# A transformer layer's hand-ordered products on one core: subtractions moved from GpSimd to VectorE, evictions spread over steps, bias stores on another queue, a rotation eight steps later

## The chip, the cores and the metric

The kernel runs on one core of a Trainium2 chip. The metric is the device time of one execution in microseconds (us), the median of several. TensorE (PE) multiplies, ScalarE (ACT) and VectorE (DVE) prepare its operands and take its results out of the accumulation banks (PSUM), GpSimd (POOL) and SyncE (SP) mostly issue transfers (DMA); POOL computes a little too.

## What is computed

One layer on 512 tokens of width 2048, batch 1, in float32:

```
h = rmsnorm(x, norm_gain)
aq, ak, av, az, iq, ik, iw, rq, rk, rv, rz, ga, gb = split(h @ w_in)
a_out = dsa_mixer(aq, ak, av, iq, ik, iw, positions, rel_bias) * silu(az)
rq = rope(rq, positions); rk = rope(rk, positions) * 128 ** -0.5
b_out = retention_mixer(rq, rk, rv, ret_gn_gain) * silu(rz)
merged = sigmoid(ga) * (a_out @ w_a_out) + sigmoid(gb) * (b_out @ w_b_out)
r = x + merged @ w_o
out = rmsnorm(r + (p @ w_ple) * sigmoid(r @ w_ple_gate), final_gain)
```

dsa_mixer is attention with 8 heads of 128, where each query uses the 128 keys that an indexer (16 heads of 64) scores highest, plus a bias by relative position. retention_mixer is retention with 8 heads of 128: scores times a decay, a state carried from chunk to chunk, and a group norm.

## The kernel before

**Operands.** TensorE multiplies in the short format fp32r. Each float32 operand is therefore split into a high and a low part, and a product is the sum of three: high by high, high by low, low by high. For a weight tile (128x1024), loaded into one of seven raw buffers, ScalarE writes the high part `wh` (L153) and VectorE the low part `wl` (L158); there are three buffers of each. Some weight tiles are the sum of two blocks: VectorE adds them (L160), or GpSimd issues a load that accumulates in the raw buffer (L119).

**Seven products for eight.** Most projections are computed as pairs of 512 columns by seven block products in place of eight. `combos` (L291) makes the seven operands of h, for 8 steps k: from two tiles xn (normalized at L707) ScalarE writes high parts (L299), the low parts come from a subtraction at L301 or L303, and four sums (L313 to L316) come ahead of them. For h the sums and the low parts of s1, s4 and a22 are GpSimd's, the other low parts VectorE's. The operands are named hs (and ha) in the rows. The parts of the first X_AWAY steps for three of the products (s2, a22, s1) go to memory and are loaded again (`x_load`).

**Order.** No scheduler decides: the program writes each engine's instructions in the order in which they are issued. `step()` is a tick, called after every three matmuls of the value products and after every two in the pairs (56 ticks a pair). `later(n, f)` runs f after n ticks. The list `bg` holds background work (making the parts of h, 48 rounds of the top-k, the masks and matmuls of the bias), of which one entry is taken each `state["rate"]` ticks.

**Stages** on the trace's clock: the indexer's queries up to 106 us; the retention values rv in two passes, 106 to 194 (`values`, L743, four banks, 16 steps; at the end of a pass ScalarE evicts the four banks with `normal`, L764, and issues a store behind each, L892); the attention's values av by seven products, 194 to 272 (`values_pair`, L909; matmuls at L947 to L949). Its results are combined by `value_out` (L896): VectorE adds or subtracts a bank and a copy (L899), ScalarE makes the high part avh, VectorE the low part avl, and ScalarE issues the stores to vd (L906). Two of the four outputs are finished at the end of the last product (`last`). Then 24 pairs, 272 to 790 us: for each of 8 heads one pair of retention query and key columns, then two pairs of merge gates. In `gate_pair` the results of a pair are copied (L246), combined (L250) and summed into `go` (L967). `finish` for a retention pair is `rotate` (L783): for queries (i = 0) and keys (i = 1) ScalarE copies the halves crosswise into `rb` (L786, L787), VectorE does two products and a sum (L788 to L790) 3, 5 and 7 ticks later; behind the keys come the steps of retention (queries times decay, L797; scores, L804; and so on) at fixed ticks, while the gate pairs run. Then the gate and attention pairs up to 1100, the attention, the output projection and the last gate.

**Bias.** The masks mk (L666) are VectorE's; the matmuls' results go through ScalarE into bev (L685), and SP issues the 32 stores to scr (L689), 8 + 4n ticks later. SP also issues most weight loads.

Of the kernel before, what the change touches and what calls it, by code (L numbers as in the profile page):

```python
# [9 lines left out]
F32 = mybir.dt.float32  # L10
F32R = mybir.dt.float32r
# [6 lines left out]
L = 512  # L18
# [17 lines left out]
def block_kernel(tc, xT, pT, posb, posq, w_in, w_v, w_ik, w_a, w_b, w_o, w_ple, w_gate,  # L36
# [4 lines left out]
    with contextlib.ExitStack() as ctx:  # L41
# [10 lines left out]
        def U(name, dt=F32):  # L52
            return up.tile([128, L], dt, name=name, tag="u")
# [121 lines left out]
        def later(n, f):  # L175
            if n <= 0:
                return f()
            tick[1] += 1
            heapq.heappush(soon, (tick[0] + n, tick[1], f))
# [108 lines left out]
                if ended[n] == 16 and n in after:  # L288
                    after[n]()

        def combos(lo, hi, name, keep=None, adder=dve, low={}):  # L291


            X = {n: [None] * 8 for n in PRODUCTS}
            T = {}

            def parts(n, k, src, sign=1.0):
                t = U(name + n, F32R)
                act.activation(t[:, LO], src, AF.Copy, scale=sign)  # L299
                if sign > 0:  # L300
                    low.get(n, dve).tensor_sub(t[:, HI], src, t[:, LO].bitcast(F32))  # L301
                else:
                    dve.scalar_tensor_tensor(t[:, HI], src, sign, t[:, LO].bitcast(F32), op0=OP.mult, op1=OP.subtract)  # L303
# [318 lines left out]
        def index_tile(m, ix):  # L622
            if m > 1:
                todo.extend(N3)
            for s in range(2):
                for t in range(1, NT):
                    todo.append(lambda s=s, t=t: index_score(2 * m + s, ix[s], t))

        for m in range(2):
            index_tile(m, ix[m])  # L630
        for m in range(2, 8):
# [49 lines left out]
        def bias_out(b, ps):  # L681
            t, gs = b
            ln = 128 * (t + 1)
            e = U("bev")
            act.activation(e[:, :ln * len(gs)], ps[:, :ln * len(gs)], AF.Copy, scale=d_back)  # L685
            for n, g in enumerate(gs):
                dst = bass.AP(tensor=scr.tensor, offset=scr.offset + 16 * (g % 8) * 1280 + TOFF[t],
                              ap=[[1280, 16], [128 * 1280, NH], [1, ln]])
                later(8 + 4 * n, lambda dst=dst, n=n: sp.dma_start(dst, e[:, ln * n:ln * n + ln]))  # L689

        def bias_banks(banks):
            for b, ps in [(b, bias_mm(b)) for b in banks]:
                bias_out(b, ps)

        x_away = [(n, k) for k in range(X_AWAY) for n in PRODUCTS[4:]]
        hd = dp.tile([len(x_away), 128, L], F32, name="hd")
        x_at = {nk: hd[i] for i, nk in enumerate(x_away)}
        xn = {}

        def xn_load(k):  # L700
            for i in (k, k + 8):
                xn[i] = U("xn")
                sp.dma_start(xn[i], xT[:, i, :])

        def xn_norm(k):
            for i in (k, k + 8):
                dve.scalar_tensor_tensor(xn[i], xn[i], ng[:, i:i + 1], R["b"], op0=OP.mult, op1=OP.mult)  # L707

        Xh, h_step = combos(lambda k: xn[k], lambda k: xn[k + 8], "h", lambda n, k: x_at.get((n, k)), pool,
                            {n: pool for n in ("s1", "s4", "a22")})  # L710
        bg.append(lambda: xn_load(0))
        for k in range(8):
            if k < 7:
                bg.append(lambda k=k: xn_load(k + 1))
            bg.append(lambda k=k: xn_norm(k))
            bg.extend([lambda k=k, i=i: h_step(k, i) for i in range(X_STEPS)])

        bg.append(lambda: state.update(rate=BG_RATES[1]))
        for r in range(16):
            for t in range(1, NT):  # L720
                bg.append(lambda r=r, t=t: topk_round(t, r == 15))
        bg.append(lambda: state.update(rate=BG_RATES[4]))
# [39 lines left out]
        def normal(ps, name, t, dt=F32):  # L762
            v = U(name, dt)
            act.activation(v, ps, AF.Copy, scale=R["nat"][:, t:t + 1])  # L764
            return v
# [6 lines left out]
        def retention(h):  # L772
# [10 lines left out]
            def rotate(i, o):  # L783
                E[i] = o
                b = U("rb")
                act.activation(b[0:64, :], o[64:128, :], AF.Copy)  # L786
# [94 lines left out]
        x_wanted = collections.deque(x_away)  # L881

        def x_load(s):
            if s >= KT - len(x_away) and x_wanted:
                n, k = x_wanted.popleft()
                Xh[n][k] = U("h" + n, F32R)
                sp.dma_start(Xh[n][k].bitcast(F32), x_at[n, k])

        for i in range(2):
            pss = values(u_rv[i], "rv", x_load if i else lambda s: None)  # L890
            for t, ps in enumerate(pss):
                act.dma_start(rd[i, t], normal(ps, "rv", t))  # L892
        state["rate"] = BG_RATES[2]


        def value_out(i, t, f, x, y):  # L896

            a = U("av")
            f(a, x, y)  # L899
            if t == NT - 1:  # L900
                vs = [(6, a)]
            else:
                h, l = split(a, "av", 2)
                vs = [(2 * t, h.bitcast(F32)), (2 * t + 1, l.bitcast(F32))]
            for j, v in vs:
                later(10 + 2 * (j % 2), lambda j=j, v=v: act.dma_start(vd[i, j], v))  # L906

        def values_pair(ids):
            banks = {}  # L909
# [4 lines left out]
                for j in range(2):  # L914
                    act.activation(E[n][j], banks[b][j], AF.Copy)

            def out(f, b, n, i, half):
                for j in range(2):
                    value_out(i, 2 * half + j, f, banks[b][j], E[n][j])
# [14 lines left out]
            for n, b in enumerate("vpqrpvp"):  # L934
                if b not in banks:
                    banks[b] = [P("ps_v" + b) for _ in range(2)]
                seq = ksteps(ids[n])
                for s, (i, k) in enumerate(seq):
                    if k == 0:
                        split_to(i + AHEAD)  # L940
                        load_to(i + AHEAD + LOADS)
                    h, l = loaded[i]
                    x = Xh[PRODUCTS[n]][s]
                    for j in range(2):
                        a, c = x[:, tok(j)], x[:, tok(2 + j)]
                        o = banks[b][j]
                        pe.matmul(o, a, h[:, k], start=(n < 4 and s == 0), stop=False, skip_group_check=True)  # L947
                        pe.matmul(o, a, l[:, k], start=False, stop=False, skip_group_check=True)
                        pe.matmul(o, c, h[:, k], start=False, stop=(s == 7), skip_group_check=True)  # L949
# [5 lines left out]
        state["rate"] = BG_RATES[3]  # L955


        sgb, sga, mbs = (dp.tile([16, 128, L], F32, name=n) for n in ("sgb", "sga", "mbs"))
# [26 lines left out]
        state["rate"] = BG_RATES[5]  # L985
        for n, u in enumerate(u_rz):
            y = B("y2")

# [402 lines left out]
AHEAD = 3  # L1391
LOADS = 5
BG_RATE = 4
BG_RATES = (2, 3, 5, 24, 16, 8)
X_AWAY = 4
HEAD = 13
WARM = 10
MANUAL = True
# [96 lines left out]
```

## Time and profile before

| | us |
|---|---|
| timed runs | 1680.54, 1682.5, 1682.78; median 1682.5 |
| profiled execution, its own time | 1680.43 |
| span of that execution | 1678.7 |
| idle of TensorE at the start (ps_ikw 1.0 and 0.2, warm 1.4) | 2.6 |
| idle of TensorE in the tail (ps_b on rl of GpSimd) | 3.5 |

TensorE's granted clock is 1.00 in all 40 slices. In the rows, a time in front is the start in us from the start of the span, then comes the duration in us, the engine and the line, the operation, result and operands, the shape, and in square brackets the idle time of the engine just before, with what ended it. A name with q (ACTq) is the engine's sequencer issuing a transfer. A grouped row has the count behind the x, then busy us and mean ns. A row of one source line has the duration in ns as least, median and greatest. The ends of matmuls are modelled; their starts are what counts.

### The profile page before, as it was taken

Reading aid. Unit: us, or ns where it says so; the run is one execution under the profiler, and the core shown is the slowest. Engines: PE = TensorE matmul, PEld = TensorE weight load, DVE = VectorE, ACT = ScalarE, POOL = GpSimd, SP = SyncE. Lnnn points to the kernel's source line nnn. Section 1 sums busy time; section 2 is a strip of 40 time slices with the busy share of each in tenths; the row PEclk is TensorE's granted clock in tenths of the full one; section 3 lists DMA queues with packets and bytes.
Section 4 is the critical chain, followed back from the end, with each engine's and each line's share of the span. In section 5 each row is a group of like instructions: output and inputs, shape, how many; then the busy total and the mean of one; then the engine's idle time right before and its main releaser. Section 6 shows DMA issues by size and latency. Waiting matters only on the chain.

```text
span 1678.7 us, 24639 instructions
## 1 busy us (share of the span) xinstructions
PE 1660.2 (99%) x9160; PEld 1441.5 (86%) x9160; DVE 1300.1 (77%) x1984; ACT 880.0 (52%) x1296; POOL 284.3 (17%) x288
## 2 busy tenths in 40 slices
PE   9999999999999999999999999999999999999997
PEld 7988788888888888888888888888888888888896
DVE  7798988988988887887887777787668887864453
ACT  7465544555555555555555555566633445463342
POOL 2116611111111111111331111100000111112222
PEclk9999999999999999999999999999999999999999
DMA  7427989788788788788998888898466788733222
GB/s 288 127 91 236 321 234 268 174 218 218 181 210 220 178 232 230 168 229 227 248 235 219 218 223 218 247 373 284 162 210 193 196 216 218 208 108 101 88 63 101
DMA packets 125577, 343.26 MB, mean 204 GB/s; under 512 B 13713, under 2 KB 25873, under 8 KB 125457
## 3 DMA queue, kind: packets, MB, share of 16 engines
q1 hardware_dynamic: 90400, 235.22, 41.5%
q0 software_dynamic: 23680, 85.99, 28.1%
q10 hardware_dynamic: 11376, 20.47, 3.4%
q8 instruction: 72, 1.18, 0.3%
q14 instruction: 49, 0.39, 0.1%
HBM read 300.21 MB, written 41.42 MB: 204 GB/s over the span
## 4 chain that ended last, share of the span: by engine, by line
PE 89%; DVE 4%; ACT 2%; issue 2%; POOL 2%; DMA 1%; ACTq 0%; SPq 0%; POOLq 0%; DVEq 0%
PE ps_p L283 23%; PE ps_v L283 15%; PE ps_r L283 8%; PE ps_q L283 7%; PE ps_w L213 3%; PE ps_w L214 3%; PE ps_w L215 3%; PE ps_pg L215 3%; PE ps_pg L213 3%; PE ps_pg L214 3%; PE ps_iq L213 1%; PE ps_iq L215 1%; PE ps_iq L214 1%; DVE wl L158 1%; ACT wh L153 1%
## 5 line engine op out<-in xcount | busy, mean ns | idle before, releaser
L158 DVE TENSOR_TENSOR wl<-wraw,wh 128x1024 fp32r<-128x1024 f32 (+2 forms) x459 | 565.4, 1241 | 156.6 <-ACT wh L153 155.4
L153 ACT ACTIVATE wh<-wraw 128x1024 fp32r<-128x1024 f32 (+2 forms) x459 | 474.3, 1043 | 257.9 <-DVE wraw L160 120.3
L119 POOL DMA_DIRECT2D wraw<-w_in x120 | 106.1, 962 | 644.1 <-DVE mk L666 245.3
L283 PE MATMUL ps_p<-hs,wh 128*128 128x512 f32 x640 | 161.1, 394 | 0.0
L246 ACT ACTIVATE e<-ps_p 128x512 f32<-128x512 f32 x144 | 86.1, 598 | 136.7 <-PE ps_p L283 134.3
L283 PEld LDWEIGHTS ps_p<-hs,wh 128*128 128x128 f32 x640 | 114.9, 189 | 21.3 <-issue 0.7
L283 PE MATMUL ps_p<-hs,wl 128*128 128x256 f32 x640 | 92.1, 284 | 1.6 <-DVE wl L158 1.6
L283 PEld LDWEIGHTS ps_p<-hs,wl 128*128 128x128 f32 x640 | 83.0, 192 | 2.1 <-DVE wl L158 2.0
L283 PE MATMUL ps_r<-hs,wh 128*128 128x512 f32 x320 | 79.9, 392 | 1.3 <-ACT wh L153 1.3
L119 POOL DMA_DIRECT2D wraw<-w_o x24 | 21.1, 945 | 348.5 <-DVE wl L158 316.5
L283 PE MATMUL ps_q<-ha,wh 128*128 128x512 f32 x320 | 80.1, 392 | 0.0
L283 PE MATMUL ps_v<-ha,wh 128*128 128x512 f32 x320 | 80.0, 392 | 0.0
L283 PE MATMUL ps_p<-ha,wh 128*128 128x512 f32 x320 | 79.3, 390 | 0.0
L283 PE MATMUL ps_v<-hs,wh 128*128 128x512 f32 x320 | 79.0, 389 | 0.0
L215 PE MATMUL ps_pg<-rh,wl 128*128 128x512 f32 x192 | 74.8, 390 | 0.0
L214 PE MATMUL ps_pg<-rl,wh 128*128 128x512 f32 x192 | 74.7, 389 | 0.0
L213 PE MATMUL ps_pg<-rh,wh 128*128 128x512 f32 x192 | 74.7, 389 | 0.0
L967 DVE TENSOR_TENSOR go<-e_t 128x256 f32<-128x256 f32 x160 | 68.0, 425 | 6.8 <-DMA bd<-go 1.2
L283 PEld LDWEIGHTS ps_r<-hs,wh 128*128 128x128 f32 x320 | 59.6, 188 | 15.8 <-ACT wh L153 2.9
L283 PEld LDWEIGHTS ps_p<-ha,wh 128*128 128x128 f32 x320 | 59.9, 188 | 12.9 <-issue 0.5
L283 PEld LDWEIGHTS ps_v<-hs,wh 128*128 128x128 f32 x320 | 60.1, 188 | 12.5
L283 PEld LDWEIGHTS ps_v<-ha,wh 128*128 128x128 f32 x320 | 59.5, 188 | 12.1
(409 smaller groups left out, 3739.9 us busy)
## 6 DMA issues: line engine op xcount, KB each, us to landing
wraw<-w_in SPq DMA_DIRECT2D x172, 512.0 KB, 5.3
wraw<-w_in POOLq DMA_DIRECT2D x120, 512.0 KB, 8.0
wraw<-w_v SPq DMA_DIRECT2D x32, 512.0 KB, 4.2
wraw<-w_o SPq DMA_DIRECT2D x32, 512.0 KB, 4.8
wraw<-w_o POOLq DMA_DIRECT2D x24, 512.0 KB, 7.0
wraw<-w_gate SPq DMA_DIRECT2D x24, 512.0 KB, 4.0
wraw<-w_b SPq DMA_DIRECT2D x16, 512.0 KB, 5.9
wraw<-w_a SPq DMA_DIRECT2D x16, 512.0 KB, 4.1
```

The costliest lines, as they stand in the source:

```text
L119: pool.dma_start(out=view(raw_tiles[r], nk, cols), in_=src[:, k0:k0 + nk, :], accum_op=OP.add)
L153: act.activation(h, raw, AF.Copy)
L158: dve.tensor_sub(l, raw, h.bitcast(F32))
L213: pe.matmul(o, h[:, k, w], a, start=(s == order[0]), stop=False)
L214: pe.matmul(o, h[:, k, w], b, start=False, stop=False)
L215: pe.matmul(o, l[:, k, w], a, start=False, stop=(s == order[-1]))
L246: act.activation(E[n], src, AF.Copy)
L283: pe.matmul(o[:, c], w[:, k], X[PRODUCTS[n]][k][:, c], start=(n < 4 and first and k == 0), stop=(ended[n] == 16), skip_group_check=True)
L967: dve.tensor_add(o[:, q], c0, c1)
```

## The change

- `combos` has VectorE do all sums and low parts, for h too.
- The evictions of rv are spread: result t of a pass is evicted and stored 3t ticks after the pass.
- In `values_pair` the four results behind the last product come at ticks 4, 10, 16 and 24 of what follows, their high parts 6 and low parts 9 ticks later, their stores 16 and 18 ticks later; high and low part lie in one big buffer (128x1280) and not in two of the 69 small ones. The earlier results have their parts 2 and 3 ticks later and stores as before.
- The 32 bias stores are issued by GpSimd, 14 + 4n ticks later and not 8 + 4n.
- The keys' rotation is 8 ticks later, the steps of retention 6 ticks later.
- X_AWAY is 5 for 4 (15 tiles for 12); the reloads start at step 3 of the second rv pass and go on in `values_pair`. The background rate of 3 between the parts of h and the top-k is gone; four empty entries stand there.

```diff
-        def combos(lo, hi, name, keep=None, adder=dve, low={}):
+        def combos(lo, hi, name, keep=None):
...
-                    low.get(n, dve).tensor_sub(t[:, HI], src, t[:, LO].bitcast(F32))
+                    dve.tensor_sub(t[:, HI], src, t[:, LO].bitcast(F32))
...
-                adder.tensor_sub(t2[:, LO], x[:, LO], x[:, HI])
-                adder.tensor_sub(t1[:, LO], x[:, HI], y[:, HI])
-                adder.tensor_sub(t1[:, HI], x[:, LO], t1[:, LO])
-                adder.tensor_sub(t2[:, HI], y[:, LO], t1[:, HI])
+                dve.tensor_sub(t2[:, LO], x[:, LO], x[:, HI])
+                dve.tensor_sub(t1[:, LO], x[:, HI], y[:, HI])
+                dve.tensor_sub(t1[:, HI], x[:, LO], t1[:, LO])
+                dve.tensor_sub(t2[:, HI], y[:, LO], t1[:, HI])
...
-                later(8 + 4 * n, lambda dst=dst, n=n: sp.dma_start(dst, e[:, ln * n:ln * n + ln]))
+                later(14 + 4 * n, lambda dst=dst, n=n: pool.dma_start(out=dst, in_=e[:, ln * n:ln * n + ln]))
...
-        Xh, h_step = combos(lambda k: xn[k], lambda k: xn[k + 8], "h", lambda n, k: x_at.get((n, k)), pool,
-                            {n: pool for n in ("s1", "s4", "a22")})
+        Xh, h_step = combos(lambda k: xn[k], lambda k: xn[k + 8], "h", lambda n, k: x_at.get((n, k)))
...
-        bg.append(lambda: state.update(rate=BG_RATES[1]))
...
+        bg.extend([lambda: None] * 4)
+        bg.extend(rounds)
...
-                act.activation(b[0:64, :], o[64:128, :], AF.Copy)
-                act.activation(b[64:128, :], o[0:64, :], AF.Copy)
-                later(3, lambda: dve.tensor_mul(o, o, ct))
-                later(5, lambda: dve.tensor_mul(b, b, st))
-                later(7, lambda: dve.tensor_add(o, o, b))
+                def swap():
+                    act.activation(b[0:64, :], o[64:128, :], AF.Copy)
+                    act.activation(b[64:128, :], o[0:64, :], AF.Copy)
+                n = 8 * i
+                later(n, swap)
+                later(n + 3, lambda: dve.tensor_mul(o, o, ct))
+                later(n + 5, lambda: dve.tensor_mul(b, b, st))
+                later(n + 7, lambda: dve.tensor_add(o, o, b))
                 if i:
                     for n, f in steps:
-                        later(n, f)
+                        later(n + 6, f)
...
-            if s >= KT - len(x_away) and x_wanted:
+            if s > 2 and x_wanted:
...
-            pss = values(u_rv[i], "rv", x_load if i else lambda s: None)
-            for t, ps in enumerate(pss):
-                act.dma_start(rd[i, t], normal(ps, "rv", t))
+            for t, ps in enumerate(values(u_rv[i], "rv", x_load if i else lambda s: None)):
+                later(3 * t, lambda i=i, t=t, ps=ps: act.dma_start(rd[i, t], normal(ps, "rv", t)))
...
+            if big:
+                b = B("avhl", F32R)
+                h, l = b[:, 0:L], b[:, L:2 * L]
             else:
-                h, l = split(a, "av", 2)
+                h, l = U("avh", F32R), U("avl", F32R)
+            later(lags[0], lambda: act.activation(h, a, AF.Copy))
+            later(lags[1], lambda: dve.tensor_sub(l, a, h.bitcast(F32)))
+            later(lags[2], lambda: store(2 * t, h.bitcast(F32)))
+            later(lags[2] + 2, lambda: store(2 * t + 1, l.bitcast(F32)))
...
-                out(dve.tensor_sub, "p", "pv", 1, 1)
-                out(dve.tensor_add, "r", "e3", 1, 0)
+                out(dve.tensor_sub, "p", "pv", 1, 1, (4, 10), (6, 9, 16), True)
+                out(dve.tensor_add, "r", "e3", 1, 0, (16, 24), (6, 9, 16), True)
...
+                    x_load(8 * n + s + 4)
...
-BG_RATES = (2, 3, 5, 24, 16, 8)
-X_AWAY = 4
+BG_RATES = (2, 5, 24, 16, 8)
+X_AWAY = 5
```

More of the change, by code (lines that the diff above doesn't have):

```diff
@@ L627, in index_tile, with xn_load, xn_norm, x_steps @@
                     todo.append(lambda s=s, t=t: index_score(2 * m + s, ix[s], t))
+        x_away = [(n, k) for k in range(X_AWAY) for n in PRODUCTS[4:]]
+        hd = dp.tile([len(x_away), 128, L], F32, name="hd")
+        x_at = {nk: hd[i] for i, nk in enumerate(x_away)}
+        xn = {}
+        def xn_load(k):
+            for i in (k, k + 8):
+                xn[i] = U("xn")
+                sp.dma_start(xn[i], xT[:, i, :])
+        def xn_norm(k):
+            for i in (k, k + 8):
+                dve.scalar_tensor_tensor(xn[i], xn[i], ng[:, i:i + 1], R["b"], op0=OP.mult, op1=OP.mult)
+        Xh, h_step = combos(lambda k: xn[k], lambda k: xn[k + 8], "h", lambda n, k: x_at.get((n, k)))
+        def x_steps(k):
+            load = [lambda: xn_load(k + 1)] if k < 7 else []
+            return load + [lambda: xn_norm(k)] + [lambda i=i: h_step(k, i) for i in range(X_STEPS)]
         for m in range(2):
@@ L889, in block_kernel, with value_out, store @@
         for i in range(2):
[L890 to L896 removed]
+            for t, ps in enumerate(values(u_rv[i], "rv", x_load if i else lambda s: None)):
+                later(3 * t, lambda i=i, t=t, ps=ps: act.dma_start(rd[i, t], normal(ps, "rv", t)))
+        state["rate"] = BG_RATES[1]
+        def value_out(i, t, f, x, y, lags, big=False):
             a = U("av")
             f(a, x, y)
+            h, l = None, None
+            def store(j, v):
+                act.dma_start(vd[i, j], v)
             if t == NT - 1:
[L901 to L906 removed]
+                return later(lags[2], lambda: store(6, a))
+            if big:
+                b = B("avhl", F32R)
+                h, l = b[:, 0:L], b[:, L:2 * L]
+            else:
+                h, l = U("avh", F32R), U("avl", F32R)
[3 more added lines that the diff above has]
+            later(lags[2] + 2, lambda: store(2 * t + 1, l.bitcast(F32)))
         def values_pair(ids):
@@ L915, in copy, with out @@
                     act.activation(E[n][j], banks[b][j], AF.Copy)
-            def out(f, b, n, i, half):
+            def out(f, b, n, i, half, at=(0, 0), *rest):
                 for j in range(2):
-                    value_out(i, 2 * half + j, f, banks[b][j], E[n][j])
+                    later(at[j], lambda j=j: value_out(i, 2 * half + j, f, banks[b][j], E[n][j], *(rest or ((2, 3, 10),))))
             def last():
                 copy("e3", "p")
-                out(dve.tensor_sub, "p", "pv", 1, 1)
-                out(dve.tensor_add, "r", "e3", 1, 0)
+                out(dve.tensor_sub, "p", "pv", 1, 1, (4, 10), (6, 9, 16), True)
+                out(dve.tensor_add, "r", "e3", 1, 0, (16, 24), (6, 9, 16), True)
             after = {
@@ L954, in block_kernel @@
         values_pair(u_av)
-        state["rate"] = BG_RATES[3]
+        state["rate"] = BG_RATES[2]
         sgb, sga, mbs = (dp.tile([16, 128, L], F32, name=n) for n in ("sgb", "sga", "mbs"))
@@ L984, in block_kernel @@
                 gate_pair(u_g[n], to(d[m:m + 2], AF.Sigmoid))
-        state["rate"] = BG_RATES[5]
+        state["rate"] = BG_RATES[4]
         for n, u in enumerate(u_rz):
```

22 lines of the change are left out of this document (3 added, 19 removed).

## The prediction

> **What bounds the kernel now.** First the page: the span and the busy times.
>
> ```profile
> span 1678.7 us, 24639 instructions
> PE 1660.2 (99%) x9160; PEld 1441.5 (86%) x9160; DVE 1300.1 (77%) x1984; ACT 880.0 (52%) x1296; POOL 284.3 (17%) x288
> ```
>
> TensorE is busy for 1660.2 of 1678.7 us. The change neither adds nor drops a matmul, so all that it can win or lose is time in which TensorE stands still; 18.5 us of it are there at all, and those at the start and in the tail (the table of before) are out of reach. So the second view is the list of what TensorE waited for, here the rows that lie between 190 and 500 us:
>
> ```profile
> PE ps_p L283 <- DVE wl L158: 1.6, 2, 1.3
> PE ps_vv L948 <- DVE wl L158: 1.5, 2, 0.8
> PE ps_vv L947 <- ACT wh L153: 1.4, 1, 1.4
> ...
> PE ps_r L283 <- ACT wh L153: 1.3, 3, 0.6
> ```
>
> The columns are microseconds in total, times, longest. That is 5.8 us in eight waits. A wait costs more than its idle time, as the timeline of TensorE at the start of the value products shows:
>
> ```profile
> 194.68 0.39 PE L947 MATMUL ps_vv<-wh,hs 128*128 128x512 f32 x1
> 195.86 0.50 PE L948 MATMUL ps_vv<-wl,hs 128*128 128x512 f32 x1 [0.79 <-DVE wl L158]
> 196.20 0.40 PE L949 MATMUL ps_vv<-wh,hs 128*128 128x512 f32 x1
> ...
> 198.29 0.40 PE L949 MATMUL ps_vv<-wh,hs 128*128 128x512 f32 x1
> 200.07 0.50 PE L947 MATMUL ps_vv<-wh,hs 128*128 128x512 f32 x1 [1.38 <-ACT wh L153]
> ```
>
> Starts are 0.23 us apart when nothing is late (2.09 us for the nine steps from 196.20 to 198.29). From 198.29 to 200.07 pass 1.78, so the wait of 1.38 takes 1.55 beyond the ordinary step, 0.17 more than its idle time, and the first step after a wait takes 0.34 (195.86 to 196.20), another 0.11. So each wait costs its idle time and some 0.28 us: 5.8 + 8 x 0.28 = **8.0 us to be had at most**. The rest of the waits, in the gate pairs:
>
> ```profile
> 284.52 0.74 PE L283 MATMUL ps_p<-hs,wl 128*128 128x256 f32 x4 [1.30 <-DVE wl L158]
> ...
> 301.16 0.74 PE L283 MATMUL ps_r<-hs,wh 128*128 128x512 f32 x2 [0.62 <-ACT wh L153]
> ...
> 306.26 1.22 PE L283 MATMUL ps_p<-hs,wl 128*128 128x256 f32 x8
> ...
> 495.39 1.21 PE L283 MATMUL ps_p<-hs,wl 128*128 128x256 f32 x8 [0.33 <-DVE wl L158]
> ```
>
> The first is in the first pair (282 to 284), the others in the pair behind a head's retention pair (301 us is head 0, 495 head 3; the other two waits of ps_r are in heads 1 and 3, 0.27 and 0.40, with 0.62 the 1.3 of the list).
>
> **The change part by part.**
>
> *Evictions of the retention values, in steps.* ScalarE before the 1.38 wait:
>
> ```profile
> 194.54 0.67 ACT L764 ACTIVATE rv<-ps_vn,r_nat 128x512 f32<-128x512 f32 x1
> 195.24 0.33 ACTq L892 DMA_DIRECT2D rd<-rv  x1
> ...
> 198.97 2.01 ACT L153 ACTIVATE wh<-wt 128x1024 fp32r<-128x1024 f32 x2 [0.40 <-ACT rv L764]
> ```
>
> Four evictions, each with its store behind it, hold ScalarE from 194.54 to 198.97; only then comes the high part that TensorE wants at 198.52, and its low part follows on VectorE. With one eviction each third tick (a tick is three matmuls, 0.69 us, so about 2 us) the high part is behind one eviction, not four, 3 x 1.1 = 3.3 us earlier. That takes the 1.38 wait and the 0.76 behind it (the rest of 1.5 less 0.79). The 0.79 at 195.86 is VectorE's, which is next. The three are 1.4 + 1.5 idle and 3 x 0.28: **-3.75**.
>
> *Sums and low parts on VectorE alone.* 56 GpSimd subtractions (128x256) move to VectorE: 4 sums and 3 low parts in each of 8 steps, all between 106 and 196 us. VectorE there:
>
> ```profile
> 106.00:194.00 88.00, 88.00 (x397) 73.19 (x396) 77.97 (x92) 47.20 (x94) 56.19 (x59) 1.00 0.70 222
> 194.00:272.00 78.00, 75.07 (x329) 61.26 (x328) 63.65 (x106) 38.19 (x45) 13.17 (x16) 1.00 0.92 251
> ```
>
> (busy time of PE, PEld, DVE, ACT, POOL, then the clock, the share of the DMA engines and GB/s). VectorE is busy for 77.97 of 88 us: there is no room for 56 more at the durations that it has now. But these durations are not its own:
>
> ```profile
> L158 DVE TENSOR_TENSOR wl<-wraw,wh 128x1024 fp32r<-128x1024 f32 x13 | 20.3, 1564 | 6.9 <-ACT wh L153 6.9
> ...
> L301 DVE TENSOR_TENSOR hs<-t,hs 128x256 fp32r<-128x256 f32 x16 | 13.9, 890 | 0.0
> L303 DVE SCALAR_TENSOR_TENSOR ha<-xn,ha 128x256 fp32r<-128x256 f32 x8 | 7.9, 990 | 0.0
> L301 DVE TENSOR_TENSOR ha<-xn,ha 128x256 fp32r<-128x256 f32 x8 | 7.1, 889 | 0.0
> ```
>
> The same line, on the same shapes, at 1240 to 1318 us, where GpSimd does nothing, and a low part of weights at 304.99:
>
> ```profile
> L301 DVE TENSOR_TENSOR ms<-t,ms x32: 414/417/419, 1240.6 to 1318.5; 128x256 fp32r<-128x256 f32 x32
> ```
>
> ```profile
> 304.99 1.22 DVE L158 TENSOR_TENSOR wl<-wraw,wh 128x1024 fp32r<-128x1024 f32 x1
> ```
>
> So beside GpSimd an operation takes 890 to 990 ns for 417, and 1564 for 1220. Without GpSimd: the four groups now take 20.3 + 13.9 + 7.9 + 7.1 = 49.2 us; then 13 x 1.22 + 32 x 0.417 = 29.2, and the 56 new ones 56 x 0.417 = 23.4. VectorE goes from 77.97 to 77.97 - 49.2 + 29.2 + 23.4 = **81.4 of 88 us**. It fits, with 3.4 us more work and no operation waiting on a GpSimd sum of 0.8 to 1.1 us; the low parts are then in time at 194.68. I cost it at nothing beyond the wait above. That it fits hangs on GpSimd's being the cause; the other end is the rival B.
>
> *Results of the value products taken out in steps.* ScalarE ahead of the wait at 284.52:
>
> ```profile
> 278.32 2.81 ACTq L906 DMA_DIRECT2D vd<-avl  x3
> ...
> 282.15 1.06 ACT L153 ACTIVATE wh<-wraw 128x1024 fp32r<-128x1024 f32 x1
> ```
>
> Three stores take 2.81 us of its queue, waiting for low parts that VectorE gives late. The high part at 282.15 and its low part (282.10 + 8 x 0.12 is when TensorE wants it) are late by that. With two ticks (0.7 us) and more between an operation and its store, and with the four results spread over 24 ticks (some 8 us) the high part comes up to 2.8 us earlier: **-1.57** (1.30 + 0.27). The same operations are done as before, in larger buffers; they lie beside the matmuls of the first pair, and the banks r and p are wanted again only by its second and later products. If they were not, one bank held for another 24 ticks would cost up to 8 us; I keep that out, since the list of waits of before has no wait for a bank.
>
> *Rotation of the keys later.*
>
> ```profile
> 361.88 0.63 ACT L786 ACTIVATE rb<-go 64x512 f32<-64x512 f32 x1 [2.63 <-DVE go L967]
> ...
> 363.18 1.06 ACT L153 ACTIVATE wh<-wraw 128x1024 fp32r<-128x1024 f32 x1
> ```
>
> ScalarE stood idle for 2.63 us for the sum of VectorE, did two copies, and only then, at 363.18, the high part for which TensorE waited in head 1. In the changed order this high part stands ahead of the copies, in the idle 2.63 us. That takes the three waits of ps_r: 1.3 + 3 x 0.28 = 2.1, and 0.1 for head 2, where the same step is late by less than the list shows: **-2.2**. The wait at 495.39 (0.33 + 0.28 = 0.6) is on VectorE's low part and can go or stay.
>
> What is late next? In head 0 the low part at 304.99 ends at 306.21 and TensorE takes it at 306.26: 0.05 to spare. When the wait of 0.62 + 0.28 goes, TensorE is there 0.9 earlier. In VectorE's changed order the same operations stand ahead of this low part as before (three of the rotation, one decay product, a weight part, a round of the top-k, only in another order; the round is one form smaller in heads 0 and 3, one larger in 1 and 2). So if VectorE's chain doesn't move up, head 0 gives back 0.85 + 0.11, head 3 keeps its 0.6 and gives back its 0.7, and heads 1 and 2 give up to 0.5 back: 2.8 in all. If the chain moves up with TensorE, 0, and the 0.6 of head 3 goes too. I take **+1.0** beyond a kept 0.6, between these ends.
>
> *Bias stores from GpSimd's queue, 6 ticks later.* 32 issues leave SP's queue, where each waits for its eviction ahead of weight loads; no TensorE wait hangs on it: 0. They now stand among GpSimd's accumulating weight loads:
>
> ```profile
> L119 POOL DMA_DIRECT2D wraw<-w_in x80: 857/882/1207, 543.4 to 1079.9; - x80
> ```
>
> 80 x 0.9 + 32 x 0.9 = 101 us in some 540: room enough, so 0 (rival C has the other end). The Trainium skill, "SBUF — State Buffer", section "Summary: rules for kernel authors", speaks against this part: a transfer issued from GpSimd has its descriptors written by GpSimd, which is starved while VectorE runs in its fast modes, and should go from ScalarE's or SP's queue. The row's 857 to 1207 beside the masks' rows bears it out by at most 0.35 us an issue; 32 x 0.35 = 11 us of GpSimd by that rule, and none of TensorE's while the accumulations have slack.
>
> *Five steps of parts to memory and back, not four; the first top-k rate dropped.* Three more tiles of 256 KB out, and back by 13 loads in the second values pass and two in the next stage: 0.5 MB more at 251 GB/s is 2 us of DMA in the 78, share 0.92 to 0.95. Cost 0; the other end is rival D. The top-k and the bias come about one round (8 to 16 us) later, far ahead of the attention at 1100: 0.
>
> **Sum**: -3.75 - 1.57 - 2.2 + 1.0 = -6.5 us; the profiled execution's 1680.4 becomes 1673.9. It lies 2.1 us under the median of the runs shown, so I take the difference from that median: 1682.5 - 6.5 = **1676.0**.
>
> **The rivals.**
> A. VectorE's low part binds in all four heads, one more operation of 128x512 late in each (4 x 0.69 = 2.8): -3.7, **1678.8**. For: 0.05 to spare in head 0. Against: same operations ahead of it.
> B. GpSimd is not what doubles VectorE's durations in that stage. Then the 56 take 890 ns like their neighbours there, 49.8 us, and VectorE has 127.8 us of work in 88: TensorE is held for 39.8, and the gains outside the stage (2.8) remain: **1719**, slower. It decides from 88 - (77.97 - 49.2) = 59.2 us for 13 weight parts and 88 subtractions: with the weight parts at 1.22, 0.49 us a subtraction. For: all four groups are slow there, and no view shows the conflict of the two engines itself. Against: the x32 row at 417.
> C. Bias stores ahead of accumulations in GpSimd's queue: 16 bursts of about 0.9 us, each past the slack: -6.5 + 14.4, **1690**. Against: 101 of 540 us.
> D. DMA: TensorE now comes 3.8 us earlier into a stage at a share of 0.92, raw weights land late, and 5.3 of the gain are lost: **1681.3**, no difference.
>
> **How the numbers follow.** A difference under 0.2% (3.4 us) can't be told from none: faster is under 1679.1, slower above 1685.9. The forecast has 0.55, A 0.20, B 0.07, C 0.05, D 0.13. Faster: 0.55 + 0.20 = 0.75; same 0.13; slower 0.12. The low end is all waits gone, 1682.5 - 8.0 - 0.6, and a run like the lowest of before: 1673.0 or a little under, 1672.5; the high end takes in A and D to 1681.5 and leaves out B and C.
>
> **What would show it.** Right: the rows of ps_vv gone from the list of waits, and that of ps_r; VectorE's low parts of weights at 1.22 and its subtractions at 417 between 106 and 194 us, busy there 81; GpSimd 57 us less, plus 29 for the stores. The prediction is wrong if VectorE's durations there stay at 890, if TensorE waits for low parts in every head, if weight loads are what ScalarE waits for from 194 to 290, or if TensorE waits show up beside the bias, from 540 on.

## The result, and the profile after

The changed kernel takes 1685.1 us (median of 18 runs, 1682.8 to 1687.8), the kernel before 1682.2 (18 runs, 1678.8 to 1685.1): a ratio of 1.0018, 95% interval 1.0011 to 1.0025. A gain of 6.5 us was forecast; 2.9 us were lost, and the time lies above the range.

The page of the changed kernel, its span and busy times:

```profile
span 1683.3 us, 24637 instructions
PE 1662.9 (99%) x9160; PEld 1444.2 (86%) x9160; DVE 1295.3 (77%) x2040; ACT 879.9 (52%) x1296; POOL 250.0 (15%) x264
```

TensorE's list of waits (us in all, times, longest), the rows of 190 to 500 us:

```profile
PE ps_rs L808 <- DVE go L794: 4.2, 4, 1.3
...
PE ps_vp L960 <- ACT wh L153: 2.8, 1, 2.8
...
PE ps_p L283 <- ACT e L246: 1.1, 1, 1.1
PE ps_vp L961 <- DVE wl L158: 0.8, 1, 0.8
```

All eight waits of before are gone. Seven others stand there: 8.9 us idle for 5.8. By the prediction's own measure (idle time and 0.28 each) that is 8.9 + 7 x 0.28 = 10.9 us for 8.0, and 1.6 us more are lost to TensorE's clock, below: 4.5 us, where the two spans differ by 4.6. The median differs by less (2.9), since the profiled execution of before lies 1.8 us under its own median.

**Between 106 and 194 us** the first part did what was worked out. The stretch, and VectorE's groups in it:

```profile
106.00:194.00 88.00, 88.00 (x397) 73.03 (x396) 74.22 (x150) 49.63 (x99) 5.45 (x6) 1.00 0.75 232
```

```profile
L158 DVE TENSOR_TENSOR wl<-wraw,wh 128x1024 fp32r<-128x1024 f32 x13 | 15.9, 1223 | 6.2 <-ACT wh L153 6.0
L301 DVE TENSOR_TENSOR hs<-t,hs 128x256 fp32r<-128x256 f32 x32 | 11.8, 416 | 0.2 <-ACT hs L299 0.2
L641 DVE SCALAR_TENSOR_TENSOR xn<-xn,g_sb,r_b 128x512 f32<-128x512 f32 x16 | 11.3, 745 | 0.0
L301 DVE TENSOR_TENSOR ha<-xn,ha 128x256 fp32r<-128x256 f32 x16 | 6.7, 420 | 0.6 <-ACT ha L299 0.2
```

Subtractions that took 890 beside GpSimd take 416, weight parts 1223 for 1564, and the normalizations, which the prediction left out, take 745 ns for 980. VectorE does 58 instructions more in 74.22 us where it took 77.97; 81.4 were forecast.

**At 206 us** stands the first new wait. ScalarE, TensorE, and the stretch behind the wait:

```profile
196.07 0.67 ACT L763 ACTIVATE rv<-ps_vn,r_nat 128x512 f32<-128x512 f32 x1
204.45 0.33 ACTq L895 DMA_DIRECT2D rd<-rv  x1
204.88 1.06 ACT L153 ACTIVATE wh<-wraw 128x1024 fp32r<-128x1024 f32 x1 [8.14 <-DMA hs<-hd]
```

```profile
205.99 0.50 PE L960 MATMUL ps_vp<-wh,ha 128*128 128x512 f32 x1 [2.76 <-ACT wh L153]
207.25 0.50 PE L961 MATMUL ps_vp<-wl,ha 128*128 128x512 f32 x1 [0.76 <-DVE wl L158]
```

```profile
208.20:211.60 3.40, 3.40 (x10) 2.62 (x9) 2.79 (x6) 2.58 (x4) 0.00 (x0) 0.50 1.04 421
```

The third eviction of the second pass ends at 196.74; its store is issued at 204.45, 7.7 us later, and the high part behind it in ScalarE's queue is late by that. What released the queue is a reload of the parts of h (hs from hd). The last row is the price on top: for 3.4 us TensorE's clock is 0.50 and its ten matmuls start 0.43 us apart, not 0.23. From 208.06 to 211.71 pass 3.65 us for nine steps that take 2.07: 1.6 us.

Why a store waits for a load is in the changed program's list of instructions (number, line, operation, and what it waits for), here ScalarE's and SyncE's:

```
213 L763 Activation rv_2139<-ps_vn_1642,r_nat_607 128x512 [waits DMAHW7_49]
214 L895 DMACopy rd_1117<-rv_2139 128x512 [waits DMAHW3_49,Activation_49]
215 L153 Activation wh_2151<-wraw_1937 128x1024 [waits DVE_49,PE_49]
...
103 L891 DMACopy hs2_2093<-hd_450 128x512 [waits DMAHW3_49,PE_49]
```

Transfers of ScalarE and SyncE share eight completion counters (DMAHW0 to 7) and take them in turn, and a transfer is issued only when the one before it on its counter has landed. Eight transfers ahead of this store, on counter 3, is a reload (number 103 of SyncE), issued at 185.63:

```profile
185.63 0.32 SPq L891 DMA_DIRECT2D hs<-hd  x1
```

It is the slowest of the reloads. Their source line, from issue to landing:

```profile
DMA to landing us min/median/max: 5.6/11.3/18.7
```

In the kernel before the same line has 4.6/9.6/12.9, for 12 reloads where there are 15 now.

**At 292 us** the same thing stands once more, with a store of the value products that waits for an earlier store of its own (the two stores of the row take 0.33 us each; 2.9 us lie between them):

```profile
287.72 3.62 ACTq L906 DMA_DIRECT2D vd<-avhl  x2
291.38 0.60 ACT L246 ACTIVATE e<-ps_p 128x512 f32<-128x512 f32 x1 [4.04 <-DMA vd<-avhl]
```

**In each of heads 0 to 3** the scores wait for the keys' rotation. TensorE and VectorE in head 0:

```profile
305.34 0.98 PE L283 MATMUL ps_r<-hs,wl 128*128 128x256 f32 x6
307.49 1.13 PE L808 MATMUL ps_rs<-go 128*128 128x128 f32 x8 [1.18 <-DVE go L794]
```

```profile
303.46 0.69 DVE L792 TENSOR_TENSOR go<-go,ct 128x512 f32<-128x512 f32 x1 [0.21 <-ACT rb L788]
304.07 1.22 DVE L158 TENSOR_TENSOR wl<-wraw,wh 128x1024 fp32r<-128x1024 f32 x1
305.20 0.69 DVE L793 TENSOR_TENSOR rb<-rb,st 128x512 f32<-128x512 f32 x1
...
306.67 0.68 DVE L794 TENSOR_TENSOR go<-go,rb 128x512 f32<-128x512 f32 x1
307.26 0.55 DVE L801 TENSOR_TENSOR qt<-go,dect 128x384 f32<-128x384 f32 x1
307.73 1.22 DVE L158 TENSOR_TENSOR wl<-wraw,wh 128x1024 fp32r<-128x1024 f32 x1
```

VectorE is busy without a break from 303.46 on; the sum of the rotation (L794), which now stands behind a weight part and a round of the top-k, ends at 307.35, and TensorE has been at the scores since 306.31.

### The profile page after: what moved, and what is told of

Its sections match the earlier page's. It is cut to its first block, busy times and chain, and to the rows that moved or that the text cites. A ratio compares the mean times of both kernels' runs of the same rounds, so it can differ in the third digit from the quotient of the medians.

```text
span 1683.3 us, 24637 instructions
## 1 busy us (share of the span) xinstructions
PE 1662.9 (99%) x9160; PEld 1444.2 (86%) x9160; DVE 1295.3 (77%) x2040; ACT 879.9 (52%) x1296; POOL 250.0 (15%) x264
## 4 chain that ended last, share of the span: by engine, by line
PE 90%; DVE 3%; DMA 3%; ACT 2%; issue 1%; POOL 0%; SPq 0%; ACTq 0%; POOLq 0%; DVEq 0%
PE ps_p L283 23%; PE ps_v L283 15%; PE ps_r L283 7%; PE ps_q L283 7%; PE ps_w L214 3%; PE ps_w L213 3%; PE ps_w L215 3%; PE ps_pg L215 3%; PE ps_pg L214 3%; PE ps_pg L213 3%; DMA hs<-hd 2%; PE ps_iq L213 1%; PE ps_iq L215 1%; PE ps_iq L214 1%; PE ps_vn L754 1%; PE ps_vn L756 1%
```

## The experiments

The theory on which they rest: the loss has three places, two where a store holds ScalarE's in-order queue until a late transfer has landed, one where a rotation was moved closer to its user. The rivals: the DMA engines are simply full and weights land late; VectorE has too much work at a pair's end in any order. All ratios are to the kernel before on the same chip. The runs are spread over four chips, so where two runs on different chips are compared, the difference is given by the medians and by the ratios.

**The rotation alone.** The kernel before with the change's `rotate` (the diff above).

> The kernel before with the keys' rotation alone as in the change (8 ticks later, retention's steps 6 later). Theory now: VectorE has no idle time from the end of the retention pair on, and the scores are brought 2 ticks nearer to the rotation than it is moved; the waits of ps_r (1.3 us) go and four waits of ps_rs for VectorE's go (about 0.5 to 1.3 each) take their place: 0 to 3 us slower than before. Theory of the prediction: the waits of ps_r go and at most a low part is late: 1 to 2 us faster. Rival: the waits of ps_rs in the changed kernel come from the delay that ScalarE's stores hand on; then this kernel has none of them.

Measured: 1686.5, ratio 1.0027 (1.0015 to 1.0039). Its waits:

```profile
PE ps_p L283 <- DVE wl L158: 2.5, 2, 2.1
PE ps_rs L809 <- DVE go L795: 2.1, 3, 0.9
PE ps_vv L953 <- DVE wl L158: 1.8, 2, 1.0
PE ps_vv L952 <- ACT wh L153: 1.8, 1, 1.8
...
PE ps_v L283 <- DVE wl L158: 0.8, 1, 0.8
```

The waits of ps_r are gone and three of ps_rs (2.1 us and 0.28 each) are there, without the spread stores: this part gains nothing by itself, and the rival, that the delay came from the stores, falls. The 5 us are more than this, though: the waits at 195 to 201 and the one in the first pair (2.13 where it was 1.30), which this part doesn't touch, are longer here, half the clock follows the latter (285 to 289 us: 0.57), and a wait of 0.8 beyond 800 us is new. How much of that is the execution's own scatter isn't shown.

**VectorE alone.** The kernel before with `combos(..., "h", keep)` without `pool`.

```diff
-        Xh, h_step = combos(lambda k: xn[k], lambda k: xn[k + 8], "h", lambda n, k: x_at.get((n, k)), pool,
-                            {n: pool for n in ("s1", "s4", "a22")})
+        Xh, h_step = combos(lambda k: xn[k], lambda k: xn[k + 8], "h", lambda n, k: x_at.get((n, k)))
```

> The kernel before with sums and low parts on VectorE alone. Theory (contention with GpSimd): VectorE's subtractions fall from 890 to about 420 ns and the weight parts from 1564 to 1220 between 106 and 194 us, VectorE is busy there for less than 82 us, the wait of 0.79 at the start of the value products goes or shrinks, the four evictions in a row still cost the other two: 0 to 1.5 us faster. Rival (durations not GpSimd's doing): VectorE over 88 us, TensorE held, 30 us and more slower.

Measured: 1680.3, ratio 0.9994 (0.9983 to 1.0006). VectorE's weight parts take 1220, its subtractions 416, and it is busy for 73.6 of the 88 us. The wait of 0.79 is gone, that of 1.38 is 0.33 and the 0.76 behind it stays, but the time can't be told from that of before.

**Evictions spread, alone.** The kernel before with `later(3 * t, ...)` for the retention values.

```diff
-            pss = values(u_rv[i], "rv", x_load if i else lambda s: None)
-            for t, ps in enumerate(pss):
-                act.dma_start(rd[i, t], normal(ps, "rv", t))
+            for t, ps in enumerate(values(u_rv[i], "rv", x_load if i else lambda s: None)):
+                later(3 * t, lambda i=i, t=t, ps=ps: act.dma_start(rd[i, t], normal(ps, "rv", t)))
```

> The kernel before with the evictions of the retention values spread over ticks, alone. Theory of the prediction: the waits of 1.38 and 0.76 us go, that of VectorE's low part stays: 2.5 us faster than before. Theory now: the stores stand in ScalarE's queue either way, spread they meet reloads that land late, so the gain is there only if the counters of these four stores belong to transfers that are through: between 2.5 us faster and 4 us slower.

Measured: 1676.9, ratio 0.9960 (0.9947 to 0.9972): 6.5 us faster, more than either expected. All its waits between 190 and 500 us:

```profile
PE ps_p L283 <- DVE wl L158: 1.4, 2, 1.1
...
PE ps_r L283 <- ACT wh L153: 1.3, 3, 0.6
```

The three waits of ps_vv are gone, VectorE's with them, although GpSimd still works beside it (VectorE's busy time in 106 to 194 us is 80.7). The prediction's -3.75 for this part is there: in the profiled executions 3.7 us are won between 194 and 201 us. Another 0.6 is won in the first 9 us, where the program is the same, so that the 6.5 of this part alone equals the 6.5 forecast for the whole change is chance. The counters of these stores belong to reloads here too, but these have landed: each store is issued right behind its eviction.

**The stores of the retention values on GpSimd's queue**, in the changed kernel.

```diff
-                later(3 * t, lambda i=i, t=t, ps=ps: act.dma_start(rd[i, t], normal(ps, "rv", t)))
+                later(3 * t, lambda i=i, t=t, ps=ps: pool.dma_start(out=rd[i, t], in_=normal(ps, "rv", t)))
```

> The changed kernel with the eight stores of the retention values issued by GpSimd and not by ScalarE. Theory now (a store in ScalarE's queue waits for the landing of an earlier transfer on the same one of eight completion counters, here a reload of the parts of h of 10 us and more, and holds the high part behind it): the waits of 2.76 and 0.76 us at 206 and the half clock behind them go, 5 to 6 us faster than the changed kernel. Rival (the weights themselves land late, since the DMA engines are full): the wait at ps_vp stays, then for a raw tile, and the time is the same.

Measured: 1678.0, ratio 0.9979 (0.9971 to 0.9988), 7 us less than the changed kernel by the medians and by the ratios. Its waits of 190 to 500 us are one row, and the reloads land as late as ever:

```profile
PE ps_rs L808 <- DVE go L794: 4.5, 4, 1.4
```

```profile
DMA to landing us min/median/max: 6.1/11.6/22.0
```

So late reloads cost nothing as long as nothing that TensorE needs is queued behind a wait for them. The rival of full DMA engines falls: they are no less full (0.96 of 194 to 272 us, 0.91 in the changed kernel), and no weight is late.

**Four steps away and not five**, in the changed kernel.

```diff
-X_AWAY = 5
+X_AWAY = 4
```

> The changed kernel with four steps of parts to memory and back, not five (12 tiles, not 15). Theory now (the store waits for a reload that is queued behind others): the last reload is issued three tiles earlier, the store of the second result of the second pass has another transfer on its counter, and the wait of 2.76 and the half clock at 206 go, with less than 1 us in its place: 4 to 6 us faster than the changed kernel. Rival (any transfer is late there, the DMA engines being full, so the spread eviction itself is at fault): a wait of 2 us and more stays.

Measured: 1678.0, ratio 0.9968 (0.9956 to 0.9980), 7 us less than the changed kernel by the medians, 8 by the ratios. Neither the wait at 206 nor that at 292 is there; what is left is the rotation's:

```profile
PE ps_rs L808 <- DVE go L794: 4.1, 4, 1.4
```

One constant, priced at nothing, is what turned the change into a loss: with 12 reloads the stores fall on other counters (the third, which was the late one, on that of a weight load), the reloads land after 12.2 us at most, and each store is issued right behind its eviction.

**The rotation 16 ticks later**, retention's steps 14, in the changed kernel.

```diff
-                n = 8 * i
+                n = 16 * i
...
-                        later(n + 6, f)
+                        later(n + 14, f)
```

> The changed kernel with the rotation of the keys 16 ticks later and retention's steps 14 later (for 8 and 6). Theory now: the low part of weights that TensorE wants next stands ahead of the rotation in VectorE's order, and the scores come behind it; the four waits of ps_rs (4.2 us and 0.28 each) go, no low part is late: 4 to 5.3 us faster than the changed kernel. Rival (VectorE's work is too much for that stretch in any order): a wait of the same size turns up at ps_p for VectorE's low part or at ps_rs again, no faster.

Measured: 1709.3, ratio 1.0165 (1.0149 to 1.0180): a miss by 28 us for the theory. SyncE, GpSimd and ScalarE behind the first head:

```profile
337.94 0.33 SPq L877 DMA_DIRECT2D yd<-yT  x1
338.36 3.11 SPq L132 DMA_DIRECT2D wraw<-w_in  x3
```

```profile
348.06 0.86 POOL L119 DMA_DIRECT2D wraw<-w_in  x1 [9.49 <-DMA wraw<-w_in]
```

```profile
358.05 2.01 ACT L153 ACTIVATE wh<-wraw 128x1024 fp32r<-128x1024 f32 x2 [5.38 <-DMA wraw<-w_in]
```

The last of retention's steps stores yT through SyncE. The store waits for yT until 337.94 (336.00 in the changed kernel), the weight loads queued behind it come after it, the accumulating load (341.99 in the changed kernel) at 348.06, and ScalarE has its raw tile at 358.05. The moved step had a transfer in a queue that weights use. TensorE waits seven times for high parts behind such a stretch (10.3 us), three times with half the clock after it: with 0.28 each and 1.6 for each half clock that is an estimated 17 of the 24 us by which this kernel is slower than the changed one. The rest is spread: the wait at 206 is 4.1, four low parts are late (3.2), and the waits of ps_rs are still there (six, 4.0 us), as the scores were again moved two ticks less than the rotation. Below, with the last step only 1 or 3 ticks later, no high part is late.

**The same, with the last steps hardly later**, and the stores on GpSimd: the lag is 17 ticks at the scores, 14 at the state's end, 12 at the values and 1 at the last step.

```diff
-                        later(n + 6, f)
+                        later(n + 17 - max(0, n - 29) // 4, f)
```

> The changed kernel with the stores of the retention values issued by GpSimd, and the keys' rotation 16 ticks later, with retention's steps 17 ticks later at first and the lag shrinking to 2 at the last, so that the store behind the last step is no later in SyncE's queue than before. Theory now (VectorE has room, but the order sets what is late; the 24 us lost with the rotation 16 ticks later came from weight loads standing behind that store in SyncE's queue): no wait of ps_rs over 0.2 us and none of ps_v for high parts, 5 us faster than with the stores alone on GpSimd, about 1672. Rival (VectorE is full at a pair's end in any order): waits of 1 us a head stay, 1677.

Measured: 1675.5, ratio 0.9950 (0.9938 to 0.9962). No wait of ps_rs; of 190 to 1100 us remains

```profile
PE ps_y L850 <- DVE state L839: 1.6, 2, 1.0
```

VectorE's work thus fits; it is its order that made the scores late. The gain over the stores alone is 2.5 us by the medians, 4.9 by the ratios, 4.0 in the profiled executions: in the direction of the theory, its size not settled.

**The rotation as in the kernel before**, the stores on GpSimd (`n = 0` and `later(n, f)`).

> The changed kernel with the stores of the retention values on GpSimd and the rotation of the keys and retention's steps as in the kernel before. Theory now: the waits of ps_rs (4.5 us and 0.28 each) go, the waits of ps_r for the high part (1.3 us in three, as before) and one of a low part come back: 2 to 4 us faster than with GpSimd's stores alone. The prediction's theory: the rotation's delay is a gain of its own, so this kernel is 2 us slower than that.

Measured: 1674.5, ratio 0.9947 (0.9935 to 0.9959), faster than with the rotation of the change by 3.5 us (medians), 5.4 (ratios) or 3.9 (profiled executions). So the rotation's delay, a gain in the prediction, is a loss here. Its only row between 190 and 500 us:

```profile
PE ps_r L283 <- ACT wh L153: 2.4, 2, 2.1
```

With the run before (the intervals overlap) this is the fastest of all kernels tried, 11 to 12 us under the changed one.

**The bias stores back on SyncE's queue**, with four steps away.

```diff
-                later(14 + 4 * n, lambda dst=dst, n=n: pool.dma_start(out=dst, in_=e[:, ln * n:ln * n + ln]))
+                later(8 + 4 * n, lambda dst=dst, n=n: sp.dma_start(dst, e[:, ln * n:ln * n + ln]))
```

> The changed kernel with four steps of parts away (as in the run of that alone) and the 32 bias stores back on SyncE's queue, 8 + 4n ticks later. Theory (the stores cost nothing on either queue, since no engine that TensorE waits for stands behind them): the same as with four steps alone, 1678, within 1.5 us. Rival (bias stores hold accumulations on GpSimd's queue, or weight loads on SyncE's): over 2 us of difference, with TensorE waits between 540 and 1060 us in one of the two.

Measured: 1677.6, ratio 0.9978 (0.9969 to 0.9987); with four steps alone it was 0.9956 to 0.9980, so no difference is shown. TensorE has no wait between 530 and 1100 us in either. The changed kernel's stores cost GpSimd 20.5 us of its own time (736 ns each); the accumulations beside them have a median of 881 ns (882 before).

**Four steps away with the later rotation**, all stores on ScalarE, and **GpSimd's stores with that rotation** (`later(n + 17 - max(0, n - 51) // 3, f)` in both).

> The changed kernel with four steps of parts away, the keys' rotation 16 ticks later and retention's steps 17 ticks later, the lag shrinking behind the value step to 3 at the last; all stores on ScalarE's queue as in the change. Theory now: neither the waits at 206 and 292 nor those of ps_rs are left, nor the two of ps_y (1.6 us) that stood when the value step had a lag of 12: 1674, 9 us below before. Rival (the late reload was only part of it, and stores in ScalarE's queue meet late landings anyway): a wait of over 1 us between 190 and 300.

> The changed kernel with the stores of the retention values on GpSimd's queue, the keys' rotation 16 ticks later and retention's steps 17 ticks later, the lag kept at 17 up to the value step (it was 14 there in the run with the shrinking lag) and 3 at the last. Theory now: the two waits of ps_y (1.6 us, and 0.28 each) go as well, nothing between 190 and 1100 us is left but an odd low part: 1 to 2 us faster than with the lag that shrinks earlier, 0.994 of before. Rival (a store in ScalarE's queue behind the value products, or a weight load behind the last step's store, is late again): no faster than that run, with a wait at ps_p for a result's copy or for high parts.

Measured: 1675.9, ratio 0.9965 (0.9953 to 0.9977), and 1678.8, ratio 0.9981 (0.9972 to 0.9990). The waits of ps_rs are gone in both. In the first the one of the first pair is back, as its rival said, with four steps away:

```profile
282.06 3.52 ACTq L906 DMA_DIRECT2D vd<-avhl  x2
285.62 0.60 ACT L246 ACTIVATE e<-ps_p 128x512 f32<-128x512 f32 x1 [4.16 <-DMA vd<-avhl]
```

The store of the value products is held until an earlier one has landed: the two stores take 3.5 us here, 2.5 us with four steps and the change's rotation, where TensorE had no wait. The time is hardly under that of four steps alone (0.9968), where 9 us below before were forecast. Whether it hurts depends on landing times, and this hazard is still in the change. The second is a miss: it has five waits in 190 to 1100 us, 1.8 us in all, and is yet slower than the one with the lag that shrinks earlier, by 3.3 us (medians) or 5.2 (ratios). Their profiled executions are 5.0 us apart: 1.1 us of that arise in the first 10 us, where the program is the same (a wait of 1.06 for a high part), 0.9 in the wait of ps_vq, and most of the rest in steps of 0.1 to 0.3 us between 300 and 800, too short for the list of waits. Why they are there stays open. So of the four kernels without the waits of ps_rs two are clearly faster than their counterpart with them, and two are not: what these waits cost, 5.3 us, is read from the waits and not confirmed by every timed run.

## Why the prediction was wrong

**What bounds the kernel** held, but for one term: only TensorE's standing still was to be had, each wait cost its idle time and about 0.28 us, and the two spans differ by what the lists of waits give, if the 1.6 us of half clock behind the longest wait are added, which no term of the prediction had.

**Evictions of the retention values, -3.75**: the mechanism and the size hold alone (ratio 0.9960), not in the change. The step that failed is "the high part is behind one eviction, not four": it counted evictions and took the store behind each for its 0.33 us. A store waits for its counter, and here the third waited for 7.7 us. The other half of it is "Five steps of parts to memory and back ... Cost 0; the other end is rival D": worked out as bytes over bandwidth, which was right (no weight was late) and not what decided. Price in the profiled execution: 2.76 + 0.76 + 2 x 0.28, and 1.6 of the clock: 5.7 us.

**VectorE alone, nothing beyond one wait**: right, and even safer than worked out (74.2 us for 81.4). Rival B is out: durations fall to 416. The Trainium skill, "SBUF — State Buffer", section "Who interferes with whom", says that a VectorE instruction with two inputs in SBUF contends with a GpSimd instruction that reads SBUF; the rows of before and after (890 and 416) agree.

**Results of the value products, -1.57**: the wait of 1.30 went, but what held ScalarE had been read wrongly. "Waiting for low parts that VectorE gives late" doesn't hold for the kernel before. Its row of three stores, one by one:

```profile
278.32 0.60 ACTq L906 DMA_DIRECT2D vd<-avl  x1
279.02 0.99 ACTq L906 DMA_DIRECT2D vd<-avl  x1
280.05 1.08 ACTq L906 DMA_DIRECT2D vd<-avl  x1
```

They stand one behind the other with at most 0.1 us between them, and the last of VectorE's low parts was done at 279.12, ahead of the last store. So they waited neither for a low part nor for a counter; each issue itself took 0.60 to 1.08 us, where the shortest of this line takes 0.33. Why these are slow isn't shown. Spread over 24 ticks a store does wait for a counter (the 2.9 us at 292): 1.1 + 0.28 = 1.4 us came back in the changed kernel.

**Rotation of the keys, -2.2, and "What is late next?", +1.0**: the three waits of ps_r went as foreseen. The failed step is the second: it looked at the next low part of weights alone. The scores were brought 6 ticks later and the rotation 8, and VectorE has a weight part and a round of the top-k between the rotation's products; four waits, 4.2 + 4 x 0.28 = 5.3 us. Rival A had the place (VectorE in all four heads) and not the instruction, and took it for 3.8 us (1.0 and 2.8).

**Bias stores, 0**: holds, by the run with them back on SyncE and by the absence of waits from 530 to 1100 us. Rival C is out: the accumulations' median was 882 ns and is 881, and the stores take 736 each.

**The cases**: rival D's outcome (no gain left) came near, by another mechanism. Slower was given 0.12 for B and C, both of which the runs exclude; the two places that took the gain were not among the rivals. The low end of the range was not worked out soundly either (1682.5 - 8.0 - 0.6 is 1673.9 and not 1673.0, and the 0.6 is already in the 8.0), but the time lies above the other end.

## What to carry to other kernels

A transfer issued by an engine that also computes is an instruction that can wait: before pricing it, read what its issue waits for (here the transfer eight places ahead on a shared counter) and what stands behind it in that queue; how late the awaited transfer lands matters then, though its bytes are few. When a producer is moved by some ticks and its user by fewer, look at the user itself and at what stands between them on the producer's engine, not only at the next thing that was nearly late. And a moved step takes its transfers along: 14 ticks on a step whose last store stands ahead of weight loads cost some 17 us.

## What the runs showed of the hardware

TensorE's clock halves after a short idle stretch, and later than it: after 2.76 us of idle time it was 0.50 from 208.2 to 211.6 us, 2.2 us behind the end of the idle stretch. In the run with the rotation alone 2.13 us of idle were enough, and in the one with GpSimd's stores and the old rotation 2.09 were not. The traces' clock records tell why. Between 10 and 1660 us there are six stretches of half speed in the kept traces, each of 3.41 us, and the full speed ahead of and between them lasts whole multiples of that (201.39 us or 59 of them ahead of 208.17). Cut along these steps of 3.41 us, the two runs show (TensorE's busy time is the first number behind the comma, the clock the third from the end):

```profile
281.69:285.10 3.41, 1.27 (x11) 1.07 (x10) 1.37 (x2) 1.97 (x3) 0.00 (x0) 1.00 1.05 392
285.10:288.51 3.41, 3.41 (x13) 3.02 (x14) 3.34 (x7) 2.01 (x2) 0.00 (x0) 0.50 0.97 335
```

```profile
292.71:296.13 3.42, 1.76 (x8) 1.12 (x6) 3.18 (x6) 1.94 (x3) 0.00 (x0) 1.00 1.01 152
296.13:299.54 3.41, 2.98 (x18) 2.64 (x19) 3.34 (x8) 2.30 (x4) 0.00 (x0) 1.00 0.73 145
```

The wait of 2.13 falls into one step, that of 2.09 is spread over two. In the six steps ahead of half speed TensorE is busy for 0.50 to 1.54 us of 3.41; in no other step of these traces for less than 1.64. So a wait of some 2 us can cost 1.6 us beyond itself or nothing, by where it falls; the wait of 1.38 in the kernel before (2.19 us busy in its step) had no such price. The Trainium skill, "TensorE: Matmul & The Clock Gate", section "Part 1: The HAM clock gate (the "warmup" mystery)", has the clock go to half after an idle window of about 3.4 us that runs freely. The length of 3.41 us agrees with it; the idle time that was enough here, 1.87 of 3.41 us, is shorter than the window.

Single executions of the same kernel scatter by up to 6 us (1678.8 to 1685.1 for the kernel before), part of it in the first 10 us of the program; a difference of 2 us or less was read from the waits or from the interval, not from two spans.
